# The backward state products of a chunked scan move to another ring of PSUM banks

## The chip, the core and the metric

The kernel runs on one core of one Trainium2 chip. The core has a matrix engine (TensorE, PE in the profile, with its weight loads listed apart as PEld), a vector engine (VectorE, DVE), a scalar engine (ScalarE, ACT), GpSimd (POOL) and SyncE (SP), which here only issues transfers. Each engine works through its own list of instructions in order, and waits on semaphores for the others. Products of TensorE land in PSUM, which the program divides into eight pages of 128 x 512 float32. The metric is the device time of one execution in microseconds (us).

## The reference

One layer of an encoder on 1024 positions of width 1024. A convolution branch and a bidirectional gated recurrence with 8 heads of 128 channels are fed from one projection, gated, merged and projected; a gated feed-forward block with a short convolution follows. The change concerns the recurrence. For each head and each direction it computes

```python
# S_t = diag(f_t) S_{t-1} + k_t v_t^T,   o_t = S_t^T q_t
new_state = exp(a_last)[..., None] * state + einsum("bhsk,bhsv->bhkv", kb * exp(a_last - a), vb)
o = einsum("bhts,bhsv->bhtv", scores, vb) + einsum("bhtk,bhkv->bhtv", qb * exp(a), state)
```

chunk by chunk, where `a` is the running sum of log f inside the chunk. The second direction is the same scan on the flipped sequence, and both outputs are added. So each chunk needs, for each direction, the product of its decayed keys with its values (`k v^T`): the state products.

## The kernel before, in words

The sequence is cut into two halves of 512 positions, and each half into four chunks of 128. A loop goes over 8 heads with two halves each: 16 half-steps, numbered here from 0 to 15. It stands between 490 and 900 us of the profile. The first small-level block below belongs to half-step 0, and the block that comes behind the states of half-step i belongs to half-step i + 1.

One half-step on TensorE is, in program order:

- `scan_levels` (L1185). The scores inside a chunk are built by levels of block size 1, 2, 4 (in `scan_base`, L1167, page `sc`), then 8 and 16 (L1209, page `ob`, matmuls at L1113), then 32 and 64 (L1216, page `sc`, matmuls at L1196, behind the small zeroing matmuls of L1218). Between the levels VectorE doubles the decayed keys `kG` and queries `qF` (L1062), and ScalarE copies rearranged operands (`A`, L1094).
- `scan_states` (L1229). The keys of both directions are transposed (L1236) and copied to `kT` by ScalarE (L1238). Then, for direction d, four matmuls (L1245) make the state products of the four chunks in a page `u`. The forward page is read by VectorE (L1251, L1253). The backward page is read by ScalarE alone, with one copy (L1263), and in the second half of a head another (L1265), into `Sb`.
- Once per head, `scan_outputs` (L1268) makes the outputs of both halves in a page `ob` each (L1286); ScalarE copies them out (L1288), sums squares (L1291), GpSimd takes the power (L519, L520), ScalarE scales (L1305), TensorE transposes back (L1312).

Between the parts of a half-step, `between` (L1374) runs pieces of an independent dense product, 1.77 pieces of six matmuls on average: products of 128 x 512 outputs, three float32r matmuls per 128 rows of depth (L148, L149, L150), each in a page `mm`, evicted by ScalarE (L730, L732). Their weights are split into two parts by ScalarE and VectorE (L124).

TensorE's order is that of the program (`manual_schedule`, L90); the other engines' lists are ordered by a scheduler. The pages are rings by tag (L98), and the page handed out is one whose last reader comes early in the program:

```python
    BANKS = {"mm": 3, "sc": 2, "tr": 2, "ob": 1}
```

So `ob` is a single page, used in turn by the levels 8 and 16, the outputs, and the backward state products. The three pages of `mm` are shared by the dense products and the transposed keys of the second direction. A new use of a page waits until the last reader of its former use is done.

Of the kernel before, what the change touches and what calls it, by code (L numbers as in the profile page):

```python
# [47 lines left out]
def tile_hybrid_encoder(  # L48
# [45 lines left out]
    def nm(s):  # L94
        uid[0] += 1
        return f"{s}_{uid[0]}"
# [3 lines left out]
    def bank(tag):  # L100
        return ps.tile([P, H], F32, tag=tag, name=nm(tag), bufs=BANKS[tag])

    def page(pool, tag, bufs, dt=F32):
        return pool.tile([P, H], dt, tag=tag, name=nm(tag), bufs=bufs)
# [962 lines left out]
    def c4(t):  # L1067
        return t.rearrange("p (c t) -> p c t", c=4)
# [160 lines left out]
    def scan_states(i, kG, v, Tt, Sf, Sb):  # L1229

        half = i % 2
        kTs = []
        for d in range(2):
            b = bank("mm" if d else "tr")
            for c in range(4):
                T.transpose(b[:, c * P : (c + 1) * P], kG[:, d, c * P : (c + 1) * P], ident)  # L1236
            kT = page(hp, "kT", 2)
            A.copy(kT, b)  # L1238
            kTs.append(kT)
        yield  # L1240
        for d in range(2):
            u = bank("ob" if d else "sc")
            for c in range(4):
                sl = slice(c * P, (c + 1) * P)
                T.matmul(u[:, sl], kTs[d][:, sl], v[:, c, :], start=True, stop=True)  # L1245
            u4 = c4(u)
            if d == 0:
                for c in range(4 if half == 0 else 3):
                    nx = Sf[half][:, c + 1, :] if c < 3 else Sf[1][:, 0, :]
                    if half == 0 and c == 0:  # L1250
                        V.tensor_copy(nx, u4[:, 0, :])  # L1251
                    else:
                        V.scalar_tensor_tensor(  # L1253
                            nx,
                            Sf[half][:, c, :],
                            Tt[:, half, 0, c : c + 1],
                            u4[:, c, :],
                            op0=ALU.mult,
                            op1=ALU.add,
                        )  # L1260
            else:

                A.copy(Sb[half][:, 0:3, :], u4[:, 1:4, :])  # L1263
                if half == 1:
                    A.copy(Sb[0][:, 3, :], u4[:, 0, :])  # L1265
        yield
# [96 lines left out]
    for h in range(NH):  # L1363
# [4 lines left out]
        for half in range(2):  # L1368
            i = 2 * h + half
            base = cur.result()  # L1370
            ahead = Base(ins) if i + 1 < NI else None
            ins = scan_inputs(i + 2) if i + 2 < NI else None

            def between(fill):  # L1374
                dense.fill(fill)
                if ahead is not None:
                    ahead.step(BASE_STEPS)
                pending.fill(1)

            S_t = hp.tile([P, 4, P], F32, tag="S", name=nm("S"), bufs=3)  # L1380
            vl = load(d_v[h][half])
            for n, _ in enumerate(scan_levels(base, S_t, Tt[:, half])):
                if n == 1:
                    b = bank("tr")
                    for c in range(4):
                        T.transpose(b[:, c * P : (c + 1) * P], vl[:, c * P : (c + 1) * P], ident)
                    v = hp.tile([P, 4, DK], F32, tag="v", name=nm("v"), bufs=3)
                    A.copy(v.rearrange("p c e -> p (c e)"), b)
                between(FILL)
            qF, kG = base[:2]  # L1390
            for _ in scan_states(i, kG, v, Tt, Sf, Sb):
                between(FILL)
            kept.append((S_t, v, qF))
            cur = ahead
# [393 lines left out]
```

## Time and profile before

| what | value |
|---|---|
| median of 3 runs | 1769.15 us (1767.91 to 1770.44) |
| profiled execution, its own time | 1768.21 us |
| its span | 1766.4 us |
| granted TensorE clock, mean | 0.996 |
| TensorE busy | 1728.3 us, 98% |
| VectorE busy | 1206.5 us, 68% |
| ScalarE busy | 808.0 us, 46% |
| the stretch 490 to 900 us: TensorE busy | 399.65 of 410 us |

The span runs from the first to the last instruction; the execution's own time has what lies around it too. Rows of the timeline give the start in us, the duration in us, the engine, the line, the operation, output <- inputs by the program's names, the size and the count; a bracket at the end gives how long the engine was idle before it and what released it. In rows of groups the durations are in ns.

### The profile page before, as it was taken

Reading aid. Unit: us, or ns where it says so; the run is one execution under the profiler, and the core shown is the slowest. Engines: PE = TensorE matmul, PEld = TensorE weight load, DVE = VectorE, ACT = ScalarE, POOL = GpSimd, SP = SyncE. Lnnn points to the kernel's source line nnn. Section 1 sums busy time; section 2 is a strip of 40 time slices with the busy share of each in tenths; the row PEclk is TensorE's granted clock in tenths of the full one; section 3 lists DMA queues with packets and bytes.
Section 4 is the critical chain, followed back from the end, with each engine's and each line's share of the span. In section 5 each row is a group of like instructions: output and inputs, shape, how many; then the busy total and the mean of one; then the engine's idle time right before and its main releaser. Section 6 shows DMA issues by size and latency. Waiting matters only on the chain.

```text
span 1766.4 us, 30281 instructions
## 1 busy us (share of the span) xinstructions
PE 1728.3 (98%) x11878; PEld 1422.8 (81%) x11878; DVE 1206.5 (68%) x1839; ACT 808.0 (46%) x1518; POOL 158.4 (9%) x171
## 2 busy tenths in 40 slices
PE   8999999999999999999999999999999999999997
PEld 6878888887888787888878888788888888888885
DVE  5599999646688877887365667666676667444455
ACT  7444443334576666776541345333444344422223
POOL 2201111100000000000000002111111111000000
PEclk9999999999999999999999999999999999999998
DMA  8777878856653443435487665677677766534233
GB/s 286 242 166 187 198 176 212 200 143 198 205 184 106 122 123 109 135 113 192 127 259 212 194 207 170 144 161 155 143 146 153 149 138 149 157 103 125 74 92 137
DMA packets 331061, 286.56 MB, mean 162 GB/s; under 512 B 24222, under 2 KB 251302, under 8 KB 330918
## 3 DMA queue, kind: packets, MB, share of 16 engines
q1 hardware_dynamic: 277878, 248.96, 45.2%
q0 software_dynamic: 43824, 34.61, 13.7%
q10 hardware_dynamic: 9216, 1.05, 0.4%
q8 instruction: 93, 1.52, 0.4%
q14 instruction: 50, 0.41, 0.1%
HBM read 189.40 MB, written 76.81 MB: 151 GB/s over the span
## 4 chain that ended last, share of the span: by engine, by line
PE 82%; ACT 5%; DVE 4%; DMA 4%; issue 3%; POOL 1%; ACTq 0%; SPq 0%; POOLq 0%; DVEq 0%
PE mm L148 19%; PE mm L150 19%; PE mm L149 19%; PE sc L148 4%; PE sc L150 4%; PE sc L149 4%; PE ob L1286 2%; PE tr L148 2%; PE tr L150 2%; PE tr L149 2%; PE sc L1113 1%; DMA tm<-d_bm 1%; POOL ors L520 1%; PE sc L1196 1%; DMA sw<-in_ffn_w_up_dram 1%
## 5 line engine op out<-in xcount | busy, mean ns | idle before, releaser
L148 PE MATMUL mm<-hx,wp 128*128 128x512 f32 x1144 | 457.5, 400 | 6.1 <-ACT su L376 2.9
L150 PE MATMUL mm<-hx,wp 128*128 128x512 f32 x1144 | 447.3, 391 | 1.6 <-DVE wp L124 1.6
L149 PE MATMUL mm<-hx,wp 128*128 128x512 f32 x1144 | 446.5, 390 | 0.0
L124 ACT CAST wp<-wr 128x1024 fp32r<-128x1024 f32 (+2 forms) x171 | 162.2, 949 | 341.4 <-PE mm L149 225.5
L148 PEld LDWEIGHTS mm<-hx,wp 128*128 128x128 f32 x1144 | 215.0, 188 | 53.0 <-ACT su L376 3.3
L150 PEld LDWEIGHTS mm<-hx,wp 128*128 128x128 f32 x1144 | 215.0, 188 | 49.8 <-DVE wp L124 3.9
L149 PEld LDWEIGHTS mm<-hx,wp 128*128 128x128 f32 x1144 | 215.4, 188 | 42.2 <-issue 0.7
L124 DVE TENSOR_TENSOR wp<-wr,wp 128x1024 fp32r<-128x1024 f32 (+2 forms) x169 | 186.7, 1105 | 83.0 <-ACT wp L124 78.8
L966 DVE SCALAR_TENSOR_TENSOR acc<-gl,v_b,acc 128x1024 f32<-128x1024 f32 x120 | 150.5, 1306 | 0.4
L1639 DVE TENSOR_TENSOR xr<-mm,xr 128x512 f32<-128x512 f32 x48 | 33.2, 692 | 72.4 <-PE mm L150 72.4
L1062 DVE TENSOR_TENSOR qF<-qF,tb 128x512 f32<-128x512 f32 x96 | 65.4, 689 | 15.5 <-ACT A L1094 14.0
L376 ACT COPY su<-mm 128x512 f32<-128x512 f32 x82 | 47.6, 581 | 61.3 <-PE mm L150 61.1
L124 ACT CAST wq<-sw 128x1024 fp32r<-128x1024 f32 x41 | 43.1, 1051 | 61.7 <-PE mm L149 40.3
L1062 DVE TENSOR_TENSOR kG<-kG,tb 128x512 f32<-128x512 f32 x96 | 65.9, 689 | 5.1 <-PE sc L1196 4.8
L1488 DVE SCALAR_TENSOR_TENSOR tm<-gp,v_a,tm 128x512 f32<-128x512 f32 x88 | 66.1, 751 | 1.9
L148 PE MATMUL mm<-hy,wp 128*128 128x512 f32 x164 | 64.5, 393 | 0.0
L148 PE MATMUL tr<-hx,wp 128*128 128x512 f32 x164 | 64.3, 392 | 0.0
L148 PE MATMUL sc<-hy,wq 128*128 128x512 f32 x164 | 64.2, 392 | 0.0
L149 PE MATMUL mm<-hy,wp 128*128 128x512 f32 x164 | 64.2, 392 | 0.0
L150 PE MATMUL sc<-hy,wq 128*128 128x512 f32 x164 | 64.2, 391 | 0.0
L150 PE MATMUL tr<-hx,wp 128*128 128x512 f32 x164 | 63.8, 389 | 0.0
L149 PE MATMUL tr<-hx,wp 128*128 128x512 f32 x164 | 63.8, 389 | 0.0
(356 smaller groups left out, 3424.2 us busy)
## 6 DMA issues: line engine op xcount, KB each, us to landing
wr<-in_w_in_dram SPq DMA_DIRECT2D x48, 512.0 KB, 5.1
wr<-in_ffn_w_up_dram SPq DMA_DIRECT2D x24, 512.0 KB, 4.0
sw<-in_ffn_w_up_dram SPq DMA_DIRECT2D x44, 256.0 KB, 3.2
d_g<-ft SPq DMA_DIRECT2D x44, 256.0 KB, 3.2
sw<-in_ffn_w_up_dram POOLq DMA_DIRECT2D x20, 512.0 KB, 8.5
sw<-in_w_in_dram SPq DMA_DIRECT2D x38, 256.0 KB
wr<-sw POOLq DMA_DIRECT2D x33, 256.0 KB, 3.4
wr<-wr POOLq DMA_DIRECT2D x33, 256.0 KB, 3.5
```

The costliest lines, as they stand in the source:

```text
L124: parts = A.copy(hi, src), eng.tensor_tensor(lo, src, hi.bitcast(F32), op=ALU.subtract)
L148: T.matmul(acc, whi[:, k, :], ahi, start=first, stop=False, skip_group_check=again)
L149: T.matmul(acc, whi[:, k, :], alo, start=False, stop=False, skip_group_check=again)
L150: T.matmul(acc, wlo[:, k, :], ahi, start=False, stop=last, skip_group_check=again)
L376: A.copy(t, acc)
L520: hold(G.tensor_tensor(dst, dst, mhalf.to_broadcast(list(dst.shape)), op=ALU.pow))
L966: V.scalar_tensor_tensor(acc, g[:, k : k + S], tap(k), acc, op0=ALU.mult, op1=ALU.add)
L1062: V.tensor_tensor(o, a, b, op=op)
L1113: T.matmul(b[g, o], A_t[:, at : at + 32], Q_t(at), start=True, stop=True)
L1286: T.matmul(o[:, sl], l, r, start=(n == 0), stop=(n == len(terms) - 1))
L1488: V.scalar_tensor_tensor(c, g[:, o + k : o + k + H], vec("fdw", k * NF + j), c, op0=ALU.mult, op1=ALU.add,)
L1639: V.tensor_tensor(xr[i][half], acc, xr[i][half], op=ALU.add)
```

## The change

In `scan_states` the page of the backward state products (d = 1) is taken from the ring `mm` instead of the single page `ob`. The matmuls, the copies out of the page and all sizes stay.

```diff
         for d in range(2):
-            u = bank("ob" if d else "sc")
+            u = bank("mm" if d else "sc")
             for c in range(4):
                 sl = slice(c * P, (c + 1) * P)
                 T.matmul(u[:, sl], kTs[d][:, sl], v[:, c, :], start=True, stop=True)
```

## The prediction

> **What bounds the kernel now.** The page first: shares of busy time and the chain that ended last.
>
> ```profile
> span 1766.4 us, 30281 instructions
> PE 1728.3 (98%) x11878; PEld 1422.8 (81%) x11878; DVE 1206.5 (68%) x1839; ACT 808.0 (46%) x1518; POOL 158.4 (9%) x171
> PE 82%; ACT 5%; DVE 4%; DMA 4%; issue 3%; POOL 1%; ACTq 0%; SPq 0%; POOLq 0%; DVEq 0%
> ```
>
> TensorE is the bound. A change of pages moves no work, so it can pay only through TensorE's waits. The view of the tile `ob` says what they are:
>
> ```profile
>   ACT Sb L1263: 10.3, 10
>   ACT Sb L1265: 2.3, 5
> ```
>
> These rows are idle time of engines that touch `ob`, in us and times: TensorE stands until ScalarE has copied the backward states out of the single page. The sum, 12.6 us, is no saving yet. It counts the idle time of a weight load and of its matmul apart, and a load of this 32-column shape is preceded by idle time even where nothing is late. So I read the first load of levels 8 and 16 in each half-step from the timeline:
>
> ```profile
> 514.71 0.35 PEld L1113 LDWEIGHTS ob<-A,A 128*32 128x32 f32 x32 [0.35 <-issue]
> 533.92 0.35 PEld L1113 LDWEIGHTS ob<-A,A 128*32 128x32 f32 x32 [1.49 <-ACT Sb L1263]
> 577.63 0.35 PEld L1113 LDWEIGHTS ob<-A,A 128*32 128x32 f32 x32 [0.35 <-ACT Sb L1263]
> 600.11 0.35 PEld L1113 LDWEIGHTS ob<-A,A 128*32 128x32 f32 x32 [0.70 <-ACT Sb L1265]
> 672.03 0.35 PEld L1113 LDWEIGHTS ob<-A,A 128*32 128x32 f32 x32 [2.88 <-ACT Sb L1263]
> 738.07 0.35 PEld L1113 LDWEIGHTS ob<-A,A 128*32 128x32 f32 x32 [0.69 <-ACT Sb L1265]
> 853.11 0.35 PEld L1113 LDWEIGHTS ob<-A,A 128*32 128x32 f32 x32 [0.70 <-ACT Sb L1263]
> ```
>
> The first row is half-step 0, which has no states before it: 0.35 us is the floor. Half-step 3 (577.63) names the copy too, but stands at the floor: the copy came just in time and cost nothing. Above the floor stand five of the sixteen: half-steps 1, 4, 7, 10 and 15, with 1.14, 0.35, 2.53, 0.34 and 0.35 us, 4.71 in all. That is what the change can take away directly.
>
> **The change, part by part.** *What it removes.* The levels' first matmul no longer waits for the copies L1263 and L1265. Its operands (`A`, L1094) are copied a half-step ahead. What counts is whether the time is kept, that is what is late next on TensorE. Half-step 7, the largest:
>
> ```profile
> 666.93 1.63 POOL L520 TENSOR_TENSOR ors<-ors,mhalf 128x8 f32<-128x8 f32 x1
> 668.60 1.28 ACT L1305 ACTIVATE tm<-tm,ors 128x128 f32<-128x128 f32 x4 [1.10 <-POOL ors L520]
> 671.52 0.46 ACT L1263 COPY Sb<-ob 128x384 f32<-128x384 f32 x1
> 672.71 0.81 ACT L1083 ACTIVATE f<-zi,lbw 128x512 f32<-128x512 f32 x1
> 672.84 0.69 DVE L1062 TENSOR_TENSOR qF<-qF,tb 128x512 f32<-128x512 f32 x1 [1.40 <-PE ob L1113]
> 675.80 0.47 PE L1196 MATMUL sc<-qF,kG 128*32 128x32 f32 x32
> 676.96 0.69 DVE L1062 TENSOR_TENSOR qF<-qF,tb 128x512 f32<-128x512 f32 x1
> 679.96 0.69 PE L1196 MATMUL sc<-qF,kG 128*64 128x64 f32 x16
> 683.92 1.05 ACT L124 CAST wp<-wr 128x1024 fp32r<-128x1024 f32 x1 [2.63 <-PE mm L150]
> 684.99 1.23 DVE L124 TENSOR_TENSOR wp<-wr,wp 128x1024 fp32r<-128x1024 f32 x1 [2.74 <-ACT wp L124]
> ```
>
> The copy is late because ScalarE's list holds it behind the output scaling (L1305), which waits for GpSimd's power. Without the wait TensorE reaches its blocks of 32 at 675.80 - 2.53 = 673.27. Their query operand is the VectorE row of 672.84, which itself waited 1.40 us for TensorE's levels; it can start at 671.44 and end at 672.13, in time. The blocks of 64 would come at 679.96 - 2.53 = 677.43; their operand ends at 676.96 + 0.69 = 677.65 if VectorE gains nothing at all. With a hand-over of 0.06 us (next fence, 604.30 against 603.55 + 0.69) that would cost 0.28, so 2.25 to 2.53 us are kept here. I take 2.53: the instruction lists of the two programs show that VectorE has three operations fewer between its `f` step (bound by the ScalarE row of 672.71) and this operand in the changed kernel. Behind it, both engines start their next stretch with a wait for TensorE, 2.63 and 2.74 us long. They follow TensorE when it comes 2.53 us sooner, and the time is kept. The other four:
>
> ```profile
> 535.10 0.69 DVE L1062 TENSOR_TENSOR qF<-qF,tb 128x512 f32<-128x512 f32 x1
> 537.67 0.47 PE L1196 MATMUL sc<-qF,kG 128*32 128x32 f32 x32
> 539.14 0.69 DVE L1062 TENSOR_TENSOR qF<-qF,tb 128x512 f32<-128x512 f32 x1
> 541.39 0.69 PE L1196 MATMUL sc<-qF,kG 128*64 128x64 f32 x16
> 545.49 0.62 ACT L1094 COPY A<-qF 128x512 f32<-128x512 f32 x1 [2.78 <-PE sc L1113]
> 603.55 0.69 DVE L1062 TENSOR_TENSOR qF<-qF,tb 128x512 f32<-128x512 f32 x1
> 604.30 0.46 PE L1196 MATMUL sc<-qF,kG 128*32 128x32 f32 x32 [0.27 <-DVE qF L1062]
> 742.16 0.46 PE L1196 MATMUL sc<-qF,kG 128*32 128x32 f32 x32 [0.18 <-DVE qF L1062]
> 853.90 0.69 DVE L124 TENSOR_TENSOR wp<-wr,wp 128x512 fp32r<-128x512 f32 x1 [3.23 <-PE ob L1113]
> ```
>
> Half-step 1: the blocks of 32 move to 537.67 - 1.14 = 536.53, their operand ends at 535.79; the blocks of 64 move to 540.25, theirs ends at 539.83. Both hold with VectorE unmoved, and ScalarE then waits 2.78 us for TensorE: 1.14 kept. Half-steps 4 and 10: the next blocks already wait for VectorE (0.27 and 0.18 us), so TensorE would only arrive sooner at a wait that ends when it did: 0 kept, 0.69 if VectorE moved as well. Half-step 15: VectorE waits 3.23 us for TensorE and follows it: 0.35 kept.
>
> *What it adds.* The page is now one of three that the dense products use, so a dense product may have to wait for the page's former reader. In the changed program 29 first matmuls of dense pages have a wait that they had not before: 15 for transposes or state products of TensorE itself, long issued, 11 for a ScalarE copy, 3 for both. The nearest rows:
>
> ```profile
> 531.08 0.61 ACT L730 ACTIVATE ev<-mm 128x512 f32<-128x512 f32 x1
> 531.23 0.48 PE L148 MATMUL mm<-hx,wp 128*128 128x512 f32 x1
> 539.94 0.39 PE L148 MATMUL mm<-hx,wp 128*128 128x512 f32 x1
> 867.69 0.58 ACT L732 COPY ev<-mm 128x512 f32<-128x512 f32 x1
> 871.72 0.39 PE L148 MATMUL mm<-hx,wp 128*128 128x512 f32 x1
> 529.30 0.40 PE L150 MATMUL mm<-hx,wp 128*128 128x512 f32 x1
> 529.53 1.06 PE L1245 MATMUL sc<-v,kT 128*128 128x128 f32 x8
> ```
>
> Behind half-step 0's states, the dense product of 531.23 takes the page of the transposed keys, and the one of 539.94 waits for the eviction that ended at 531.69: 8 us of slack. The tightest, in the tail, is 871.72 against 868.27: 3.45 us. A wait already met costs nothing visible: L1245 has one, and starts 0.23 us behind the last dense matmul, the ordinary spacing. So 0; the upper end, with the ring handing out the page just finished, is the third rival. Nothing is moved on GpSimd's or SyncE's lists; ScalarE's and VectorE's differ in places around 674 to 681 us and at the scan's end, by reordering alone: a loss of up to the 0.28 above, a gain of up to the 0.69 of half-steps 4 and 10; taken as 0.
>
> *Sum.* 1.14 + 0 + 2.53 + 0 + 0.35 = 4.02 us. The profiled execution's 1768.21 becomes 1764.2. It lies 0.94 below the median; taken from the median 1769.15 the forecast is 1765.1 us. Bounds: 0 kept (1769.15) and all 4.71 kept (1764.4).
>
> The dense ring is where a rule of the Trainium skill speaks against the change. "Perfetto Trace Analysis", section "Optimizing Tensor Performance", wants independent matmul groups to rotate through different PSUM banks, so that one's eviction overlaps the next group's matmuls. Lending one of three banks to the states leaves less of that. By this rule the eviction would show in front of dense products, as worked out in the third rival (1773 us); the slack of 3.45 and 8 us in the rows above says it stays hidden.
>
> **Rivals.** *Second, only part is kept (1766.4).* Where the wait goes, the chain from GpSimd's power through ScalarE and VectorE decides. Half-step 5 shows it:
>
> ```profile
> 621.03 1.64 POOL L520 TENSOR_TENSOR ors<-ors,mhalf 128x8 f32<-128x8 f32 x1
> 632.78 0.69 PE L1196 MATMUL sc<-qF,kG 128*64 128x64 f32 x16 [0.58 <-DVE qF L1062]
> ```
>
> From the power to the blocks of 64, VectorE-bound, it is 11.75 us there; in half-step 7 it is 679.96 - 666.93 = 13.03. Were 11.75 the least, half-step 7 would give 1.28, the sum 2.77, the time 1766.4. Against it: half-step 7's operand was itself late by a wait for TensorE.
>
> *Third, the dense ring stalls (about 1773, slower).* If the page handed out behind the states is the one of the dense product just finished, its first matmul waits for the eviction: 531.69 against 531.23, with the hand-over 0.52 us, in each of 16 half-steps: 8 us against 4.0 gained. It decides from 0.25 us per half-step on. Against it: the waits listed above name earlier readers.
>
> *Fourth, nothing changes (1769).* The wait was only the last of several that end together. Against it: in half-step 7, TensorE's row names only the copy, and ScalarE's timeline between 668.60 and that row has no operand copy.
>
> *Fifth, more is kept (1763 or less)*, if half-steps 4 and 10 and further VectorE waits move too.
>
> **How the numbers follow.** 0.62 for the forecast, 0.22 for the second, 0.08 for the third, 0.04 each for the fourth and fifth. 0.2% is 3.5 us, about what a measurement of this kernel tells from no change; the bound for faster is 1765.6, only 0.5 above the forecast. Of the forecast's 0.62 I put 0.53 beyond it, with 0.04 of the fifth and 0.02 of the second: 0.59 faster. Slower is the third rival, 0.08; the rest, 0.33, is within. The range 1763.2 to 1768.2 holds the first two cases with a us of scatter, and leaves out the third and fourth.
>
> **What would show it.** Right: loads of levels 8 and 16 at 0.35 us in every half-step with no `Sb` release; TensorE's busy time unchanged; the blocks of 64 of half-step 7 some 10.5 us behind GpSimd's power. Wrong: a row of L148 released by an eviction or by `Sb` (third), more idle time in front of L1196 released by VectorE (second), or another copy named in front of L1113 (fourth).

## The result and the profile after

The changed kernel takes 1765.2 us (median of 22 runs, 1762.12 to 1770.1); the kernel before took 1768.81 us in 22 runs beside it. The ratio is 0.9981, with a 95% interval of 0.9973 to 0.9989, that is 1.9 to 4.8 us less; the forecast was 1765.1. The single runs of one kernel spread over 8 us, twice the effect. So the median gives the size, and the cause has to be read from the rows.

The profile page of the changed kernel, the three rows that answer to those of before:

```profile
span 1764.2 us, 30274 instructions
PE 1730.1 (98%) x11878; PEld 1423.2 (81%) x11878; DVE 1206.5 (68%) x1839; ACT 808.1 (46%) x1518; POOL 158.8 (9%) x171
PE 78%; DMA 7%; DVE 5%; ACT 5%; issue 3%; POOL 1%; ACTq 0%; SPq 0%; POOLq 0%; DVEq 0%
```

Nothing moved between engines; every busy time but TensorE's is the same within 0.4 us, and TensorE's 1.8 us more is no added work: with the same 11878 matmuls its busy time runs from 1726.4 to 1730.7 us over the twelve profiles of this document. The share of TensorE in the chain fell from 82% to 78%, although TensorE waits less: the chain follows one path of one execution, so its shares are not used further.

Two of the idle rows of the view of the tile `ob`, after:

```profile
  PE ob L1286: 28.5, 16
  issue: 5.1, 15
```

The releases by `Sb` (10.3 and 2.3 us before) are gone, and most of the 15 pieces under "issue", 0.34 us on average, are the floor: the 0.35 us that stand before such a load where nothing is late. The first load of levels 8 and 16, in the half-steps that were shown of before:

```profile
515.62 0.35 PEld L1113 LDWEIGHTS ob<-A,A 128*32 128x32 f32 x32 [0.35 <-ACT ev L730]
533.70 0.35 PEld L1113 LDWEIGHTS ob<-A,A 128*32 128x32 f32 x32 [0.36 <-issue]
577.41 0.35 PEld L1113 LDWEIGHTS ob<-A,A 128*32 128x32 f32 x32 [0.35 <-issue]
598.24 0.35 PEld L1113 LDWEIGHTS ob<-A,A 128*32 128x32 f32 x32 [0.35 <-issue]
668.14 0.35 PEld L1113 LDWEIGHTS ob<-A,A 128*32 128x32 f32 x32 [0.36 <-issue]
734.70 0.35 PEld L1113 LDWEIGHTS ob<-A,A 128*32 128x32 f32 x32 [0.35 <-issue]
849.76 0.35 PEld L1113 LDWEIGHTS ob<-A,A 128*32 128x32 f32 x32 [0.35 <-issue]
```

All sixteen loads, these seven and the other nine, stand at 0.35 or 0.36 us, the floor. The places of the rows give what was kept: half-step 1 comes 533.70 - 515.62 = 18.08 us behind half-step 0, against 533.92 - 514.71 = 19.21 before, 1.13 less.

Half-step 7 after, in the timeline, and the two places where the waits went:

```profile
665.55 1.64 POOL L520 TENSOR_TENSOR ors<-ors,mhalf 128x8 f32<-128x8 f32 x1
667.22 1.28 ACT L1305 ACTIVATE tm<-tm,ors 128x128 f32<-128x128 f32 x4 [1.10 <-POOL ors L520]
670.16 0.46 ACT L1263 COPY Sb<-mm 128x384 f32<-128x384 f32 x1
671.91 0.47 PE L1196 MATMUL sc<-qF,kG 128*32 128x32 f32 x32
676.07 0.69 PE L1196 MATMUL sc<-qF,kG 128*64 128x64 f32 x16
602.78 0.46 PE L1196 MATMUL sc<-qF,kG 128*32 128x32 f32 x32 [0.62 <-DVE qF L1062]
739.15 0.46 PE L1196 MATMUL sc<-qF,kG 128*32 128x32 f32 x32 [0.53 <-DVE qF L1062]
```

The copy out of the states' page is as late as it was (670.16, 4.6 us behind GpSimd's power; before 671.52 and 4.6 as well). But the levels no longer ask for it: they start at 668.14, two us ahead of the copy. The blocks of 64 stand 10.52 us behind the power, against 13.03. In half-steps 4 and 10 the blocks of 32 wait for VectorE's query operand, 0.62 and 0.53 us where it was 0.27 and 0.18: the gain of 0.35 us that each had at its levels is given back there.

### The profile page after: what moved, and what is told of

Read it like the earlier page. It is cut to its first block, busy times and chain, and to the rows that moved or that the text cites. A ratio compares the mean times of both kernels' runs of the same rounds, so it can differ in the third digit from the quotient of the medians.

```text
span 1764.2 us, 30274 instructions
## 1 busy us (share of the span) xinstructions
PE 1730.1 (98%) x11878; PEld 1423.2 (81%) x11878; DVE 1206.5 (68%) x1839; ACT 808.1 (46%) x1518; POOL 158.8 (9%) x171
## 4 chain that ended last, share of the span: by engine, by line
PE 78%; DMA 7%; DVE 5%; ACT 5%; issue 3%; POOL 1%; ACTq 0%; SPq 0%; POOLq 0%; DVEq 0%
PE mm L148 18%; PE mm L150 18%; PE mm L149 18%; PE sc L148 3%; PE sc L150 3%; PE sc L149 3%; PE ob L1286 2%; PE tr L148 2%; PE tr L150 2%; PE tr L149 2%; DMA wr<-wr 1%; PE sc L1113 1%; DMA wr<-sw 1%; DVE acc L966 1%; DVE wp L124 1%
## 5 line engine op out<-in xcount | busy, mean ns | idle before, releaser
L148 PE MATMUL mm<-hx,wp 128*128 128x512 f32 x1144 | 457.9, 400 | 6.3 <-ACT su L376 2.8
L148 PEld LDWEIGHTS mm<-hx,wp 128*128 128x128 f32 x1144 | 215.2, 188 | 53.9 <-ACT su L376 4.0
L148 PE MATMUL mm<-hy,wp 128*128 128x512 f32 x164 | 64.5, 393 | 0.0
L148 PE MATMUL tr<-hx,wp 128*128 128x512 f32 x164 | 64.3, 392 | 0.0
L148 PE MATMUL sc<-hy,wq 128*128 128x512 f32 x164 | 64.2, 392 | 0.0
```

The lines of the kernel that those rows point to most:

```text
L148: T.matmul(acc, whi[:, k, :], ahi, start=first, stop=False, skip_group_check=again)
```

## The experiments

The runs of one kernel scatter by more than most effects here, so each experiment is read twice: by its ratio, and by the length of the scan in its profile. The scan's stretch runs from the first load of levels in half-step 0 to the last forward state product. The first rows stand above and in the prediction; the last ones, before and after, are

```profile
867.20 1.05 PE L1245 MATMUL sc<-v,kT 128*128 128x128 f32 x8
863.87 1.05 PE L1245 MATMUL sc<-v,kT 128*128 128x128 f32 x8
```

So the stretch is 867.20 - 514.71 = 352.49 us before and 863.87 - 515.62 = 348.25 us after. Each stretch is that of one execution, and waits in front of L1245 move by up to 1.3 us between kernels whose edits do not touch that place (last part of the account below), so a difference of about a us between two stretches says nothing alone. Each ratio is against the kernel before in runs beside it, whose median was between 1767.32 and 1768.81 us; medians of different rows compare only roughly.

| kernel | median us | ratio, 95% interval | stretch against before |
|---|---|---|---|
| the change | 1765.2 | 0.9981 [0.9973, 0.9989] | -4.24 |
| only half-step 7's states moved | 1765.17 | 0.998 [0.9967, 0.9993] | -1.81 |
| all but those | 1768.92 | 1.0004 [0.999, 1.0019] | -1.03 |
| page of the transposes | 1764.18 | 0.9969 [0.9958, 0.9981] | -3.49 |
| both directions' states in `mm` | 1765.88 | 0.9981 [0.9969, 0.9993] | -2.94 |
| page `ob`, copy on VectorE | 1762.92 | 0.9978 [0.9968, 0.9987] | -4.19 |
| page `ob`, scaling on GpSimd | 1757.73 | 0.9935 [0.9916, 0.9955] | -8.43 |
| page `mm`, scaling on GpSimd | 1755.24 | 0.9926 [0.9908, 0.9943] | -10.96 |
| page `tr`, scaling on GpSimd | 1755.11 | 0.9935 [0.9918, 0.9951] | -10.82 |
| page `mm`, score transfers on SyncE | 1761.47 | 0.9957 [0.9942, 0.9972] | -7.08 |
| page `mm`, both moves | 1756.35 | 0.9928 [0.9908, 0.9948] | -11.35 |

### Half-step 7 alone, and all but half-step 7

The states in front of half-step 7 are those of the loop's step 6. First they alone take the page of `mm`:

```diff
-            u = bank("ob" if d else "sc")
+            u = bank(("mm" if i == 6 else "ob") if d else "sc")
```

> The state products of one half-step alone (the first half of head 3, whose copy held the levels of half-step 7 for 2.88 us) go to the dense ring; the other fifteen stay in the single page. I measure the stretch of the scan from the first load of the levels 8 and 16 in half-step 0 to the forward state products of the last half-step: 352.49 us before, 348.25 with the full change. Theory 'sum of five waits': the load of half-step 7 falls from 2.88 to the floor of 0.35, those of half-steps 1, 4, 10 and 15 stay (1.49, 0.70, 0.69, 0.70 us); the stretch falls by 2.3 to 2.5 us, the time by the same, ratio about 0.9986. Rival 'the chain from GpSimd's power decides': the wait moves to the blocks of 64 (L1196), 1.3 us kept. Rival 'the gain is elsewhere' (the reordering on VectorE and ScalarE or run scatter): the stretch falls by less than 1 us.

Then all the others:

```diff
-            u = bank("ob" if d else "sc")
+            u = bank(("ob" if i == 6 else "mm") if d else "sc")
```

> The complement: all half-steps but that one use the dense ring. No other engine's list changes order. Theory 'sum of five waits': half-step 7 keeps its 2.88 us, half-steps 1, 4, 10 and 15 go to the floor; kept are 1.14 + 0.35 = 1.49 us (half-steps 4 and 10 give theirs back at L1196); ratio about 0.9992. With the run before the two parts add up to the full change. Rival 'the chain decides' expects the same here. Rival 'gain elsewhere': the fall of the stretch is not 1.5 us but nearer to the full change or to nothing.

The weight loads of levels in the first kernel, half-steps 1, 4, 7 and 8:

```profile
534.56 0.35 PEld L1113 LDWEIGHTS ob<-A,A 128*32 128x32 f32 x32 [1.21 <-ACT Sb L1263]
600.81 0.35 PEld L1113 LDWEIGHTS ob<-A,A 128*32 128x32 f32 x32 [0.70 <-ACT Sb L1265]
670.27 0.35 PEld L1113 LDWEIGHTS ob<-A,A 128*32 128x32 f32 x32 [0.36 <-issue]
690.98 0.35 PEld L1113 LDWEIGHTS ob<-A,A 128*32 128x32 f32 x32 [0.69 <-ACT Sb L1265]
```

and in the second, half-step 7:

```profile
670.47 0.35 PEld L1113 LDWEIGHTS ob<-A,A 128*32 128x32 f32 x32 [2.88 <-ACT Sb L1263]
```

The waits can be taken away half-step by half-step: each of the two kernels removes its own and leaves the others (half-step 1 keeps 1.21 of 1.49 us in the first). TensorE's rows gain 2.52 us at half-step 7 in the first kernel, and 1.13 and 0.35 at half-steps 1 and 15 in the second, as expected.

The stretches do not add up as expected. They fall by 1.81 and 1.03 us instead of 2.3 to 2.5 and 1.49, and together by 2.84, not by 4.24. In the first kernel a single page passes a delay on: half-step 7 came earlier, and half-step 8, which had been at the floor, then waits 0.34 us more than that for its copy. Another 0.31 us are lost in front of the states of half-step 9, and 0.35 at the same place in the second kernel. In the profile of the full change, 1.30 us were gained in front of the states of half-step 3 and 0.84 lost in front of those of half-step 9. What moves these places is taken up in the account of the prediction; it is not the page.

By the runs, half-step 7 alone gives a gain as large as the whole change (0.998 against 0.9981, the intervals overlap), and the others alone give none that can be told; the 0.9992 that were expected of them lie inside their interval too.

### Other rings

The page of the transposes instead, and then both directions' states in `mm`:

```diff
-            u = bank("ob" if d else "sc")
+            u = bank("tr" if d else "sc")
```

> The backward state products go to the two pages of the transposes (tr) instead, all half-steps. If what pays is that the small levels no longer share a page with the copied states, the stretch falls as with the dense ring, by 4.0 to 4.3 us, and no new wait stands in front of the transposes L1236, L1386 or L1312. If the room in the dense ring is what matters, or a two-page ring is too tight, the transposes wait for the copy (L1263) or the state products for a copy of keys (L1238), and the gain is under 2 us.

```diff
-            u = bank("ob" if d else "sc")
+            u = bank("mm")
```

> Both directions' state products go to the dense ring: its load in the scan rises from about 4.2 to 5.2 pages per half-step, and the forward page is held longer, until VectorE has read all chunks (L1251, L1253). Theory 'the dense ring has room' (slack of 3.45 us and more): time within 0.2% of the changed kernel, no row of L148 released by Sb, Sf or an eviction. Rival 'the ring is at its limit': rows of L148 or L1245 released by VectorE's Sf or by an eviction, some tenths of a us in most half-steps, 3 to 8 us in all, slower than the changed kernel and about as the kernel before or slower.

With the transposes' pair all loads of levels are at the floor again, no transpose waits for a state copy, and half-steps 1, 7 and 15 gain 1.13, 2.52 and 0.35 us as with `mm`: what counts is to leave the single page, and the pair does as well as `mm`. The stretch falls by 3.49 us, less than the 4.0 to 4.3 expected; 0.39 of that went in front of the states of half-step 9, the place named above. With both directions in `mm` the levels gain the same, but at one place the ring is at its limit, which the theory of enough room had ruled out; by the runs it takes as long as the changed kernel, as that theory had it, and the rival's 3 to 8 us do not show. Half-step 10, ScalarE's copies and the dense product behind the states:

```profile
729.12 1.86 PEld L1245 LDWEIGHTS mm<-v,kT 128*128 128x128 f32 x16 [1.25 <-ACT kT L1238]
733.51 0.47 ACT L1263 COPY Sb<-mm 128x384 f32<-128x384 f32 x1
733.88 0.27 ACT L1265 COPY Sb<-mm 128x128 f32<-128x128 f32 x1
734.20 0.19 PEld L148 LDWEIGHTS mm<-hx,wp 128*128 128x128 f32 x1 [2.07 <-ACT Sb L1265]
735.79 0.35 PEld L1113 LDWEIGHTS ob<-A,A 128*32 128x32 f32 x32 [0.36 <-issue]
```

A dense product (L148) waits 2.07 us for the copy of the states. From the states to the levels it takes 735.79 - 729.12 = 6.67 us, in the changed kernel 734.70 - 729.98 = 4.72 (729.98 is a row of the last fence), so 1.95 us are lost; 0.69 of them come back at the blocks of 32, which no longer wait for VectorE there. A row of L148 released by `Sb` is the sign that the prediction gave for the third rival. It comes once in sixteen half-steps, and only with a second page lent. The rule of the Trainium skill that the prediction weighed ("Perfetto Trace Analysis", section "Optimizing Tensor Performance", independent groups rotate through different banks) agrees with this row; with one page lent, as in the change, no trace here shows its price.

### Who makes the copy late

Half-step 7's copy was late, by the prediction, because ScalarE's list holds it behind the scaling. Three kernels test the list. First, the single page stays, and the copy moves to VectorE's list:

```diff
-                A.copy(Sb[half][:, 0:3, :], u4[:, 1:4, :])
+                V.tensor_copy(Sb[half][:, 0:3, :], u4[:, 1:4, :])
                 if half == 1:
-                    A.copy(Sb[0][:, 3, :], u4[:, 0, :])
+                    V.tensor_copy(Sb[0][:, 3, :], u4[:, 0, :])
```

> The single page stays; the copies of the backward states (L1263, L1265) go from ScalarE's list to VectorE's. Theory (the page costs what the copy's place in an engine's list makes it cost): in half-step 7 the copy runs behind VectorE's state updates L1253 (669.78 before) and ends about 1.7 us sooner, so that the 2.88 us in front of L1113 fall to about 1.2; half-step 1 keeps about 1.4 of 1.49. The scan's stretch falls by 1.5 to 3 us, the time is 1766 to 1767.5 us. Rival (VectorE cannot carry it): its 10 us of added copies show as waits of L1196 for VectorE, the stretch does not fall, and the time is 1769 us or more.

VectorE's rows and the levels of half-step 7:

```profile
667.59 1.11 DVE L1253 SCALAR_TENSOR_TENSOR Sf<-Sf,Tt,sc 128x128 f32<-128x128 f32 x3
668.62 0.55 DVE L1263 COPY Sb<-ob 128x384 f32<-128x384 f32 x1
669.22 0.35 PEld L1113 LDWEIGHTS ob<-A,A 128*32 128x32 f32 x32 [1.16 <-DVE Sb L1263]
690.44 0.43 PE L1113 MATMUL ob<-A,A 128*32 128x32 f32 x29 [0.86 <-DVE Sb L1265]
```

The wait of 2.88 us is 1.16, as the theory gave; half-step 1 keeps 1.18 where about 1.4 was expected. The stretch falls by 4.19 us, more than the theory's 1.5 to 3. Of that, 1.72 us come in front of the states of half-step 3, where the wait for the keys is gone: the four transfers took 2.58 us there in this execution, as in that of the change, against 3.89 before, and ScalarE has less to do (busy 801.4 us instead of 808.0). The rival's sign, waits of L1196 for VectorE, does not show: they fall from 3.6 to 2.3 us. But VectorE's list too makes a copy late: at half-step 8, which stood at the floor before, the levels wait for its second copy (last row) and come 0.90 us later.

Second and third, the scaling L1305 goes from ScalarE to GpSimd, on the kernel before and on the changed one:

```diff
-                A.activation(
-                    ons[half][:, sl], ons[half][:, sl], AF.Copy, scale=rs[:, half, c : c + 1]
+                G.tensor_scalar(
+                    ons[half][:, sl], ons[half][:, sl], rs[:, half, c : c + 1], None, op0=ALU.mult
                 )
```

> The kernel before, with the output scaling (L1305, 64 multiplications of 128 x 128) done by GpSimd instead of ScalarE. ScalarE then never waits for GpSimd's power, and its list can reach the state copies sooner. Theory 'the copy is late because ScalarE's list holds it behind the scaling': with the single page kept, the 2.88 us of half-step 7 and the 0.70 of half-steps 4, 10 and 15 fall to the floor of 0.35; the 1.49 of half-step 1, before which no head has been scaled, stays. The scan's stretch (352.49 us before) falls by 2.5 us or more. Rival 'the copy is late because ScalarE is simply loaded, or because of the order around it': half-step 7 keeps over 1 us. The scheduler reorders ScalarE and VectorE around this edit, so the sum is less sure than the rows.

> The changed kernel with the scaling on GpSimd. The waits for the copy are gone already; what is left of the chain from GpSimd's power are TensorE's waits at L1196 for VectorE (0.72, 0.58, 0.82, 0.63, 1.09 and 1.12 us in the profile of the changed kernel, 0.35 of each the floor or less). If ScalarE's wait for the power causes them, they shrink and the stretch (348.25 us) falls by 1 to 3 us more. If VectorE's own load causes them, they stay and the time is that of the changed kernel within 0.1%. GpSimd's multiplications could make the transposes back (L1312) late: then rows of L1312 are released by GpSimd.

The single page with the scaling away, half-steps 1, 4 and 7:

```profile
533.07 0.35 PEld L1113 LDWEIGHTS ob<-A,A 128*32 128x32 f32 x32 [1.27 <-ACT Sb L1263]
597.04 0.35 PEld L1113 LDWEIGHTS ob<-A,A 128*32 128x32 f32 x32 [0.35 <-ACT Sb L1265]
662.73 1.06 PE L1245 MATMUL ob<-v,kT 128*128 128x128 f32 x8
663.56 0.64 ACT L1081 ACTIVATE kG<-zi 128x512 f32<-128x512 f32 x1
665.31 0.64 ACT L1094 COPY A<-kG 128x512 f32<-128x512 f32 x1
665.84 0.49 ACT L1263 COPY Sb<-ob 128x384 f32<-128x384 f32 x1
666.38 0.35 PEld L1113 LDWEIGHTS ob<-A,A 128*32 128x32 f32 x32 [1.64 <-ACT Sb L1263]
```

Half-step 7's wait falls from 2.88 to 1.64 us, those of half-steps 4, 10 and 15 go to the floor, and half-step 1, which has no scaling in front of it, keeps 1.27 of 1.49. The theory had half-step 7 at the floor as well; here its rival was right, that over 1 us stays. So the scaling, which the prediction named as the cause, makes about half of half-step 7's lateness. The other half is the order of ScalarE's list: the states are done at 662.73 + 1.06 = 663.79, and the four operations from L1081 to L1094 run ahead of the copy at 665.84. The scheduler ordered this list anew, so the halves are rough; but in the kernel before, too, three activations on the inputs of a later half-step (L1082, L1081 and L1083, 1.74 us from 669.78 on) stand between the scaling and the copy at 671.52. The Trainium skill says that a gap which repeats on the engine that should be saturated can mean that there is not enough PSUM for the next tile ("Perfetto Trace Analysis", section "Optimization Strategy"). That fits the remedy here, but not the pattern: the page was shared in the same way in all sixteen half-steps, and TensorE lost time in the five where the list was late.

With the scaling on GpSimd the change is worth 10.96 - 8.43 = 2.53 us of stretch instead of 4.24. By the runs the two are not told apart (0.9926 and 0.9935 with overlapping intervals). The larger gain is the scaling itself; on the changed kernel it was expected to take 1 to 3 us more off the stretch and took 6.72. The groups of the scan (from 500 to 880 us) of the changed kernel:

```profile
L1305 ACT ACTIVATE tm<-tm,ors 128x128 f32<-128x128 f32 x56 | 18.8, 392 | 9.3 <-POOL ors L520 9.3
L1196 PE MATMUL sc<-qF,kG 128*32 128x32 f32 (+1 forms) x768 | 18.4, 208 | 4.3 <-DVE qF L1062 4.3
L1245 PE MATMUL sc<-v,kT 128*128 128x128 f32 x128 | 17.1, 276 | 1.5 <-ACT kT L1238 1.5
```

and with the scaling on GpSimd as well:

```profile
L1305 POOL TENSOR_SCALAR tm<-tm,ors 128x128 f32<-128x128 f32 x64 | 67.5, 1073 | 0.8
L1196 PE MATMUL sc<-qF,kG 128*32 128x32 f32 (+1 forms) x768 | 18.4, 208 | 0.2 <-DVE qF L1062 0.2
L1245 PE MATMUL sc<-v,kT 128*128 128x128 f32 x128 | 16.9, 275 | 0.0
```

By these rows one scaling takes 1073 ns on GpSimd instead of 392 on ScalarE, and the kernel is 10 us faster. ScalarE no longer stands 9.3 us in front of GpSimd's result, and TensorE's remaining waits, 4.3 us for VectorE's operand and 1.5 for the keys, go with it but for 0.2. That is most of the 6.72 us of the stretch. The rest of the 10 us lies outside the stretch, and its cause was not looked for.

The same scaling with the states on the transposes' page:

```diff
-            u = bank("ob" if d else "sc")
+            u = bank("tr" if d else "sc")
```

> The states' products on a page of the transposes' pair, and the output scaling L1305 on GpSimd. Theory (any page other than the single one removes the wait, and the rest of the gain of the scaling does not depend on the page): the scan's stretch falls by 10.5 to 11 us against the kernel before, as with the dense page and the same scaling (10.96), all loads of levels 8 and 16 stand at 0.35 us, and the time is 1754 to 1757 us. Rival (the transposes' two pages become the limit once ScalarE is earlier): a transpose (L1236, L1312 or L1386) waits for the states' copy, 0.3 us or more in several half-steps, and the time is 1758 us or more.

It comes out as with `mm` and as the theory had it (1755.11 and 1755.24 us, stretches 0.14 us apart), and no transpose waits for a state copy. Between these two rings no difference shows here either.

### The score transfers

Four small transfers per half-step (`S` <- `D`, L1226) are issued from ScalarE's list. They go to SyncE's, on the changed kernel, and then together with the scaling's move:

```diff
-            nc.scalar.dma_start(S_t[g : g + 32, :, g : g + 32], D_t[g : g + 32])
+            nc.sync.dma_start(S_t[g : g + 32, :, g : g + 32], D_t[g : g + 32])
```

> The changed kernel with the four small transfers S<-D per half-step (L1226) issued by SyncE instead of ScalarE. On ScalarE their issue takes 44.12 us of the scan in the profile of the changed kernel, between 2.55 and 3.90 us per half-step, and the two waits of the state products for the key copies (L1245, 1.92 and 0.43 us) stand where this issue was longest or in line behind it. If that is their cause, L1245 falls to no idle time and the stretch falls by about 1.5 to 2.5 us. Rival: SyncE's list is in order too, and a wait for S and D at its head delays the loads of z, q, v and weights: then L1386, L1113 of page sc or L150 wait for transfers, and the time is not better or worse by some us.

> The changed kernel with both moves: scaling on GpSimd, the small transfers on SyncE. If both causes hold, the scan has hardly any idle time of TensorE left beside the floor: the stretch falls by 3 to 5 us below 348.25, ratio to the kernel before about 0.996. If VectorE's load is what stands behind L1196, 1 to 2.5 us. If SyncE's list is delayed, slower than the changed kernel.

On the changed kernel the move is worth 7.08 - 4.24 = 2.84 us of stretch, a little over the 1.5 to 2.5 expected, and the waits of L1245 for the keys are gone:

```profile
L1245 PE MATMUL sc<-v,kT 128*128 128x128 f32 x128 | 16.9, 274 | 0.0
L1196 PE MATMUL sc<-qF,kG 128*32 128x32 f32 (+1 forms) x768 | 18.4, 208 | 3.2 <-DVE qF L1062 3.2
```

On top of the scaling's move it adds nothing that can be told (0.9928 against 0.9926): GpSimd's scaling had already taken those waits. Both moves together take the stretch 7.11 us below that of the change, where 3 to 5 were expected. The four kernels with the scaling on GpSimd lie 11 to 13 us under the kernel before, and their intervals overlap.

## Why the prediction was right

*The floor.* Right. All sixteen loads stand at 0.35 or 0.36 us once the page is free, so 12.6 us of listed idle time were 4.71 us of real waits.

*The five half-steps.* By the places of TensorE's rows, half-steps 1, 7 and 15 gain 1.13, 2.52 and 0.35 us, against 1.14, 2.53 and 0.35 forecast. Half-steps 4 and 10 gain 0.35 and 0.36 at the levels and give back 0.34 and 0.35 at the blocks of 32 behind them, as forecast. The sum is 4.02. What they give back is the added idle time in front of L1196 (4.3 us against 3.6 before) that the prediction had listed as a sign of the second rival; nearly all of it stands at these two places, where the forecast kept nothing, and none at half-step 7.

*Half-step 7 between 2.25 and 2.53.* The upper end held. The blocks of 64 stand 10.52 us behind GpSimd's power, so the 11.75 us of the second rival were no least distance. The row names no wait for VectorE, so the 0.28 us left open were not lost. Wrong in part is the cause that the prediction gave for the late copy: the scaling is only about half of it, and its fence left out the three activations behind the scaling. The sum did not need that cause, since the change leaves the copy as late as it was.

*The added waits at nothing.* Right for this change: between 490 and 910 us no row of L148 names an eviction or a state copy. The slack is not large everywhere: one more page lent, and a stall of 1.95 us comes.

*What the stretch gained beyond the sum*, 0.22 us, is not the change's. Two places in front of L1245 differ by -1.30 and +0.84 us; the rest is small, +0.17 at the blocks of half-step 6 without a recorded wait the largest. The two places, the states of half-steps 3 and 9, before:

```profile
588.17 3.89 ACTq L1226 DMA_DIRECT2D S<-D  x4
595.04 0.97 PEld L1245 LDWEIGHTS sc<-v,kT 128*128 128x128 f32 x8 [1.72 <-ACT kT L1238]
727.97 3.08 ACTq L1226 DMA_DIRECT2D S<-D  x4
732.99 0.97 PEld L1245 LDWEIGHTS sc<-v,kT 128*128 128x128 f32 x8 [1.08 <-ACT kT L1238]
```

and after:

```profile
587.97 2.58 ACTq L1226 DMA_DIRECT2D S<-D  x4
593.52 0.97 PEld L1245 LDWEIGHTS sc<-v,kT 128*128 128x128 f32 x8 [0.43 <-ACT kT L1238]
724.13 3.90 ACTq L1226 DMA_DIRECT2D S<-D  x4
729.98 0.97 PEld L1245 LDWEIGHTS sc<-v,kT 128*128 128x128 f32 x8 [1.92 <-ACT kT L1238]
```

The issue of the four transfers took 1.31 us less at the first place and 0.82 more at the second, and TensorE's wait for the keys, which ScalarE copies behind them, moved by 1.29 and 0.84. The page does not decide it. With the states of half-step 3 in `mm` the four transfers took 2.58 us at the first place in the changed kernel and 3.84 in the kernel that moves all but half-step 7's; in the single page they took 3.89 before, 3.94 with only half-step 7's moved, and 2.58 with the copy on VectorE. No kernel was profiled twice, so how far one kernel varies at this place is not known.

Outside the stretch the two profiles differ by 2.0 us the other way (0.9 ahead of it, 1.1 behind). What makes that was not found; over the twelve profiles the time outside the stretch runs from 1410.9 to 1417.8 us. The spans, 2.2 us apart, therefore say little about the gain.

*The time.* That 1765.2 us meet the forecast of 1765.1 is in part luck. The forecast took 4.02 us from 1769.15; beside the changed kernel the kernel before stood at 1768.81, and the gain was 3.6 us by the medians, 3.4 by the ratio. The interval of 1.9 to 4.8 us holds the second rival's 2.77 as well, so it is the rows that decide between the two.

*The chances.* Faster is supported: the interval ends at 0.9989. That the gain is over 0.2% is not settled, since the interval holds 0.998.

## What to carry to other kernels

A wait for a page is to be measured against the floor of the same instruction where nothing is late, and then followed to the next wait on that engine: here 12.6 us of idle time became 4.71 us of waits and 4.02 us of gain. A single page shared between two uses couples the matrix engine to the place of a copy in another engine's list. Another page removes the coupling, but the list stays late, and here it was worth more to take the waiting operation off that list (8.4 us of stretch with the single page kept) than to leave the page (4.2 us). An operation that waits long for another engine's result can be better placed on that engine, even where it takes nearly three times as long there.

## What was not expected of the hardware

The issue of four equal transfers from ScalarE's queue took 2.55 us in some half-steps and up to 3.94 in others, and at the same half-step 2.58 in the execution of one kernel and 3.84 in that of another with the same page there. TensorE's wait for the keys, which are copied behind them in ScalarE's list, moved by nearly the difference. On SyncE's queue four transfers took 2.52 to 3.86 us in one execution, so the spread is not ScalarE's alone. What makes it was not tried.
